# A streaming-encoder block on one Trainium2 core: where the moving operands begin in SBUF

## The chip, the core and the metric

One core of a Trainium2 chip runs the whole block as one program. The engines are TensorE (PE, with its weight loads listed as PEld), VectorE (DVE), ScalarE (ACT), GpSimd (POOL) and SyncE (SP), which issues most transfers. Each has its own queue of instructions, and they meet at semaphores. The metric is the device time of one execution in microseconds.

## The reference, cut to what matters

One layer on x of 512 tokens by 1024 features, all in float32:

```python
x = x + 0.5 * swiglu(rms_norm(x, ffn1_norm), w1, w3, w2)          # D_FF = 2816
h = rms_norm(x, mix_norm);  p = h @ w_in                           # 5288 columns
y_a = rwkv7_mixer(token_shift(p_rwkv), ...) @ rwkv_proj            # 8 heads x 64, delta rule
y_b = fox_mixer(p_fox, ...) @ fox_proj                             # 8 heads x 64, forgetting attention
x = x + (sigmoid(g_a) * y_a + sigmoid(g_b) * y_b) @ w_out
x = x + 0.5 * swiglu(rms_norm(x, ffn2_norm), v1, v3, v2)
out = rms_norm(x, final_norm)
# swiglu(h, w1, w3, w2) = (silu(h @ w1) * (h @ w3)) @ w2
```

## The kernel before, in words

Activations lie transposed: a tile holds 128 features by 512 tokens, so one product has a weight tile of 128 x 128 as the stationary operand and 512 columns of activations as the moving one. To keep float32 accuracy, every weight and every activation is split in two float32r parts, hi and lo, and `mm3` (L124 to L127) makes three products of each pair: weight hi with activation hi (L125), weight hi with activation lo (L126), weight lo with activation hi (L127).

Weights come through a ring of buffers: `raw` (three, filled by SP's queue, 512 KB at a time), `whi` (two, made by ACT, L117) and `wlo` (two, made by DVE, L118). These buffers and the normed activations `xh`, `xl` begin at byte 288 modulo 512 in each partition. One weight buffer holds eight tiles of 512 bytes per partition, so that every 128-column tile in it begins at 288 modulo 512 too.

The stages, by the names of the PSUM tiles that the products write:

- FFN 1 (`ffn`): `pa` and `pb` are h @ w1 and h @ w3 for each of 22 blocks of features, with `xh`/`xl` moving. DVE and ACT make silu(a) * b and split it into `hh` and `hl`. Then `pd`, the second product with w2: per output block m, 22 weight tiles with `hh`/`hl` moving, 66 products.
- The mixer: `pl` are the low-rank codes (72 and 96 weight columns instead of 128), `pk` the RWKV columns, `pgt` the gates, `pv` the values (here the weights move), `pq` the attention's q and k. The delta rule runs in chunks of 32 tokens as small fp32 products (`gp`, `xps`, `ups`, `sps`, `yps`) between the larger ones. Attention uses `lp`. LayerNorm over heads uses `yc` and `pg`.
- `ppj` (function `proj`): first the attention's output `yh`/`yl` by fox_proj, then the RWKV output `ya` by rwkv_proj, 96 products each. DVE gates the results, in the slots `G` and `ga`, with gate values that POOL's queue brings back from DRAM (`gsave`, L910 and L918). `pw` is the merged result `mh`/`ml` by w_out, 192 products; its sum goes to the reloaded residual `xS`.
- FFN 2 as FFN 1; its last output block is worked in two halves of 256 tokens with the weight buffers `ownh`/`ownl`, so that the final norm of one half runs beside the other (`ot`, `os`).

Buffers are laid out by pools, one behind the other in each partition: the constants `cp` first, then `xp` (activations), `wp` (weights), `tp` (temporaries), and behind these either `hp` (`hh`, `hl`) or the mixer's `rp` and `sp`. Pools opened with `side="right"` (`vtp`, `t2`) grow down from the other end. The order of the work is set by the tile framework's scheduler from the program text.

Where the operands begin, modulo 512, in the program before:

| buffers | used in | begin at |
|---|---|---|
| `whi`, `wlo`, `own`, `xh`, `xl` | weights everywhere; moving in `pa`, `pb`, `pk`, `pgt`, `pq`, `pl` | 288 |
| `hh`, `hl` | moving in `pd` | 416 |
| `yh`, `yl` | moving in the first `ppj` | 480 |
| `ya` | moving in the second `ppj` | 320 |
| `mh`, `ml` | moving in `pw` | 320 |
| `qa`, `kb`, `klc`, `vt`, `tr`, `pts` | attention | 480 (every second head's slice of `vt`: 224) |
| `la`, from which the first `qb` is made | attention, beside `klc` | 64 |
| `G`, `BK`, `RD`, `Tall`, `V4` (and the slots `ga`) | the recurrence, gates | 320 (every second chunk of `G` and `BK`: 64) |

Of the kernel before, what the change touches and what calls it, by code (L numbers as in the profile page):

```python
# [9 lines left out]
F32 = mybir.dt.float32  # L10
# [8 lines left out]
P = 128  # L19
T = 512  # L20
# [5 lines left out]
NP = DA // P  # L26
C = 32
NC = T // C
NB = T // P
# [6 lines left out]
PAR_W0, PAR_A0, PAR_KK, PAR_KA, PAR_RK, PAR_LG, PAR_LB = 38, 42, 46, 50, 54, 58, 62  # L36
PAR_Q, PAR_K, PAR_F = 66, 67, 68
PAR_N = 69

COL_W = 3 * DA  # L40
COL_G = COL_W + 64
# [9 lines left out]
def kernel(  # L51
# [7 lines left out]
    dve, act, pool, pe = nc.vector, nc.scalar, nc.gpsimd, nc.tensor  # L59

    cp = ctx.enter_context(tc.tile_pool(name="cp", bufs=1))
    xp = ctx.enter_context(tc.tile_pool(name="xp", bufs=1))
    wp = ctx.enter_context(tc.tile_pool(name="wp", bufs=2))
    tp = ctx.enter_context(tc.tile_pool(name="tp", bufs=4))
# [5 lines left out]
    def bank(name, pool_=None):  # L70
        pool_ = pool_ or pm
        return pool_.tile([P, T], F32, tag="b", name=name)

    def tmp(name, shape=(P, T), dt=F32, tag="t", **kw):
        return tp.tile(list(shape), dt, tag=tag, name=name, **kw)
# [3 lines left out]
    make_identity(nc, ident)  # L79
    identb = cp.tile([P, P], BF16, name="identb")  # L80
    dve.tensor_copy(identb[:], ident[:])
    ones = cp.tile([P, P], F32, name="ones")
    dve.memset(ones[:], 1.0)
    onesr = cp.tile([P, P], F32R, name="onesr")
    dve.tensor_copy(onesr[:], ones[:])
    bones = tmp("bones", (P, P))
    dve.memset(bones[:], 0.0)
    dve.memset(bones[0:64, 0:64], 1.0)
# [115 lines left out]

    par = cp.tile([P, PAR_N], F32, name="par")

# [5 lines left out]
    nc.scalar.dma_start(g1[:], ffn1_norm[0].rearrange("(a b) -> a b", b=P))  # L212
    warm = bank("warm", pf)
    for _ in range(8):
        pe.matmul(warm[:, 0:P], ones[:], ones[:], start=True, stop=True)
    gtp = bank("gtp", pr)
    pe.transpose(gtp[:, 0:8], g1[:], ident[0:8, 0:8])
    dve.tensor_copy(par[:, 0:8], gtp[:, 0:8])
# [28 lines left out]
    tc.keep_in_program_order(pin)  # L247
    rows = rtp.tile([PAR_N, P], F32, name="rows")
    loraw = rtp.tile([P, DA], F32, name="loraw")
# [45 lines left out]
    def place_params():  # L295
        ptp = bank("ptp")
        pe.transpose(ptp[:, 0:PAR_N], rows[:], ident[0:PAR_N, 0:PAR_N])
        dve.tensor_copy(par[:, 8:PAR_N], ptp[:, 8:PAR_N])
        dve.tensor_scalar(par[:, PAR_Q:PAR_Q + 1], par[:, PAR_Q:PAR_Q + 1], 0.125, None, op0=ALU.mult)
# [79 lines left out]
    with ExitStack() as mx:  # L379
        rp = mx.enter_context(tc.tile_pool(name="rp", bufs=1))  # L380
# [13 lines left out]

        nka = rp.tile([P, NP], F32, name="nka")
        dve.tensor_scalar(nka[:], par[:, PAR_KA:PAR_KA + NP], -1.0, None, op0=ALU.mult)
        tiny = rp.tile([P, 2], F32, name="tiny")
        dve.memset(tiny[:, 0:1], 1e-24)
        dve.memset(tiny[:, 1:2], -1e-24)
        omu = rp.tile([P, PAR_W0 - PAR_MU], F32, name="omu")  # L400
        dve.tensor_scalar(omu[:], par[:, PAR_MU:PAR_W0], -1.0, 1.0, op0=ALU.mult, op1=ALU.add)

        def shifted(o, src, rows, mu):
            act.activation(o[0:rows, :], src[0:rows, :], AF.Copy, scale=omu[0:rows, mu - PAR_MU:mu - PAR_MU + 1])
            dve.scalar_tensor_tensor(o[0:rows, 1:T], src[0:rows, 0:T - 1], pc(mu)[0:rows, :], o[0:rows, 1:T],
                                     op0=ALU.mult, op1=ALU.add)
# [47 lines left out]
        xctx.close()  # L454
        fctx = ExitStack()
        vtp = fctx.enter_context(tc.tile_pool(name="vtp", bufs=1, side="right"))
        pctx = ExitStack()
        t2 = pctx.enter_context(tc.tile_pool(name="t2", bufs=1, side="right"))
        cmask = t2.tile([P, T], F32, name="cmask")
        pool.memset(cmask[:], 1.0)  # L460
        pool.memset(cmask[:].rearrange("p (c t) -> p c t", t=C)[:, :, 0:1], 0.0)

        PC = rp.tile([P, NP, NC], F32, name="PC")
        Ld = dp.tile([P, C, C], F32, name="Ld")
        Td = dp.tile([P, C, C], F32, name="Td")
        V4 = rp.tile([P, NP, T], F32, name="V4", tag="V4")
# [37 lines left out]
        def step(p):  # L504
# [21 lines left out]
            with tc.issue_after(logs.ins):  # L526
                act.activation(Pi[:], cz[:], AF.Exp, scale=DEC)
                act.activation(Pp[:, :, 1:C + 1], ch(cz), AF.Exp, scale=-DEC)
            pool.tensor_copy(PC[:, p, :], Pp[:, :, C])
            dve.tensor_tensor(BK[:, :, 1, :], ch(k), ch(Pi), op=ALU.mult)  # L530
# [87 lines left out]
        for i in range(2):  # L618
            for q in range(2):
                o = i * 64 + q * C  # L620
# [6 lines left out]
        def half(q):  # L627
            return slice(q * 64, (q + 1) * 64)
# [49 lines left out]
        vt = []  # L678
# [6 lines left out]
                    mm3(vps[b][:], mix.hi[kk][:, bs], mix.lo[kk][:, bs], wh[:, k, :], wl[:, k, :],  # L685
                        kk == 0, kk == KD - 1)
        for b in range(NB):
            o = vtp.tile([P, T], F32, name=f"vt{b}", tag=f"vt{b}")
            act.activation(o[:], vps[b][:], AF.Copy, scale=rc[:, b:b + 1])
            vt.append(o)  # L690
        plain_gate(NP)
# [10 lines left out]
        for q in range(2):  # L702
            pool.memset(Rs[0][half(q), :, q, :], 0.0)
            for i in range(4):
                o = (1 - q) * 64
# [21 lines left out]
        for c in range(NC):  # L727
# [3 lines left out]
            for p, q in heads():  # L731
                o = (p // 2) * 64 + q * C
# [12 lines left out]
            if c + 1 < NC:  # L745
# [3 lines left out]
                for q in range(2):  # L749
                    decay = dve.tensor_tensor(Rn[half(q), :, q, :], sps[half(q)],  # L750
                                      PC[half(q), :, c:c + 1].broadcast_to([64, NP, 64]), op=ALU.mult)
            holes += [hx, hx, hu, hu, hs, hs]
# [21 lines left out]
        for q in range(2):  # L774
            o = (1 - q) * 64
            pool.memset(f32(klc[q][:]), 0.0)
            dve.tensor_copy(klc[q][o:o + 8, :], fz[FR, :])
        for q in range(2):
            o = (1 - q) * 64
# [8 lines left out]
        for p in range(NP):  # L788
            qp, kp = qks[p]
            qa = [t2.tile([P, T], F32R, tag=f"qa{q}", name=f"qa{q}") for q in range(2)]  # L790
            kb = [t2.tile([P, T], F32R, tag=f"kb{q}", name=f"kb{q}") for q in range(2)]


            for q in range(2):
                h_, g_ = half(q), half(1 - q)
                h = 2 * p + q
                act.copy(qa[q][h_, :], qp[h_, :])
                dve.tensor_tensor(qa[q][g_, :], qp[h_, :], f32(qa[q][h_, :]), op=ALU.subtract)
                dve.tensor_copy(kb[q][h_, :], kp[h_, :])
                dve.tensor_copy(kb[q][g_, :], kp[h_, :])  # L800
                dve.tensor_tensor(klc[q][h_, :], kp[h_, :], f32(kb[q][h_, :]), op=ALU.subtract)
                act.copy(qb[q][h_, :], qp[h_, :])
                dve.tensor_copy(qb[q][g_, :], sel[g_, h:h + 1].broadcast_to([64, T]))
            mx_ = [tp.tile([P, 2 * NB], F32, tag=f"mx{q}", name=f"mx{q}", bufs=2) for q in range(2)]
            for i, bl in enumerate(((0, 1), (2,), (3,))):
                at = {b: sum(c + 1 for c in bl[:j]) * P for j, b in enumerate(bl)}
                w = sum(b + 1 for b in bl) * P
                lps, trs = [], []
                for q in range(2):
                    lp = pf.tile([P, T], F32, tag="b", name="lp")  # L810
                    lps.append(lp)
                    for b in bl:
                        n, bs = (b + 1) * P, slice(b * P, (b + 1) * P)
                        l = lp[:, at[b]:at[b] + n]
                        pe.matmul(l, qa[q][:, bs], kb[q][:, 0:n], start=True, stop=False)
                        pe.matmul(l, qb[q][:, bs], klc[q][:, 0:n], start=False, stop=False)
                        pe.matmul(l[:, b * P:n], identb[:], dmask[:], start=False, stop=True)
                for q in range(2):
                    pt, mx = pts[:, q], mx_[q]
                    for b in bl:  # L820
                        n, mb = (b + 1) * P, mx[:, b:b + 1]
                        l = lps[q][:, at[b]:at[b] + n]
                        dve.tensor_reduce(mb, l, axis=AX.X, op=ALU.max, negate=True)
                        act.activation(pt[:, at[b]:at[b] + n], l, AF.Exp, bias=mb, accum_out=mx[:, NB + b:NB + b + 1])
                    sb_ = mx[:, NB + bl[0]:NB + bl[-1] + 1]
                    dve.reciprocal(sb_, sb_)
                    for b in bl:
                        v = pt[:, at[b]:at[b] + (b + 1) * P]
                        dve.tensor_scalar(v, v, mx[:, NB + b:NB + b + 1], None, op0=ALU.mult)
                for q in range(2):  # L830
                    tpp = lps[q]
                    for k in range(w // P):
                        pe.transpose(tpp[:, k * P:(k + 1) * P], pts[:, q, k * P:(k + 1) * P], ident[:])
                    tr = t2.tile([P, T], F32, tag="tr", name="tr", bufs=2)
                    act.copy(tr[:, 0:w], tpp[:, 0:w])
                    trs.append(tr)

                av = lps[1]
                for j, b in enumerate(bl):
                    for k in range(b + 1):  # L840
                        o = at[b] + k * P
                        for q in range(2):
                            h = 2 * p + q
                            pe.matmul(av[half(q), j * P:(j + 1) * P], vt[k][:, h * 64:(h + 1) * 64],
                                      trs[q][:, o:o + P], start=k == 0, stop=k == b)
                dve.tensor_copy(qp[:, bl[0] * P:(bl[-1] + 1) * P], av[:, 0:len(bl) * P])
                if p == 0 and i < 2:
                    load_qk(i + 2, holes)
                    norm_qk(i + 2)
                elif 3 * p + i < 3 * NP - 1:  # L850
                    early(3 * p - 2 + i)
            yb.append(qp)
# [50 lines left out]
        for p in range(NP):  # L903
            o = vtp.tile([P, T], F32R, name=f"yh{p}", tag=f"vt{p}")
# [119 lines left out]
```

## Time and profile before

| | |
|---|---|
| median of three timed runs | 1213.7 us |
| lowest and highest of them | 1209.55 and 1213.95 us |
| span of the profiled execution, first to last instruction | 1210.2 us |
| mean granted TensorE clock in it | 0.992 |
| TensorE busy | 1184.5 us, 98% |
| DVE, ACT, POOL busy | 665.2, 458.1, 100.5 us |
| moved by DMA | 122.54 MB, 101 GB/s in the mean |

The page and the views give times from the start of the span; for the profiled execution there is no other time than this span. "Busy" of TensorE is the union of its products: a product of 512 columns stands with some 390 ns from its start to its modelled end, while the next one starts some 230 ns after it. The time that a stream of products costs is therefore read from start to start. The granted clock stands as a share of full speed.

### The profile page before, as it was taken

The page shows a single profiled execution, that of the slowest core. Times are in us where ns is not written, and L with a number is a line of the kernel's source. Part 1 is how long each engine was busy: PE and PEld are TensorE (multiplying, and loading weights), DVE is VectorE, ACT ScalarE, POOL GpSimd, SP SyncE. Part 2 cuts the span into 40 slices and gives each one's busy share as a digit, 9 for nine tenths or more (in the row PEclk, how much of TensorE's full clock was granted, in tenths as well). Part 3 has the DMA queues.
Part 4 walks back from the last instruction along what each step waited for, and adds up shares of the span by engine and source line. Part 5 has one row for each costly group of instructions (what it writes and reads, how often), then busy time and mean ns, then how long its engine had stood idle before and what let it go on. Part 6 is the DMA issues. An engine that isn't in the chain of part 4 may idle for free.

```text
span 1210.2 us, 15874 instructions
## 1 busy us (share of the span) xinstructions
PE 1184.5 (98%) x6334; PEld 955.1 (79%) x6334; DVE 665.2 (55%) x993; ACT 458.1 (38%) x739; POOL 100.5 (8%) x144
## 2 busy tenths in 40 slices
PE   8999999999999999999999999999999999999997
PEld 6788888888887788887667777678888888888887
DVE  7454555443443688776766666865554445443232
ACT  5222222222222854445867655523322222222221
POOL 4100000001111111321000011111000000000110
PEclk9999999999999999999999999999999999999999
DMA  6233233333334234345113235532333333323331
GB/s 186 73 95 105 87 105 88 104 95 108 107 111 106 76 104 124 109 135 131 36 36 102 63 97 163 178 106 87 103 102 92 100 104 88 104 80 96 96 96 70
DMA packets 208152, 122.54 MB, mean 101 GB/s; under 512 B 9902, under 2 KB 200430, under 8 KB 208078
## 3 DMA queue, kind: packets, MB, share of 16 engines
q1 hardware_dynamic: 202078, 108.67, 31.1%
q0 software_dynamic: 3760, 12.06, 3.2%
q8 instruction: 50, 0.82, 0.3%
q10 hardware_dynamic: 2240, 0.79, 0.3%
q14 instruction: 24, 0.20, 0.1%
HBM read 110.82 MB, written 10.68 MB: 100 GB/s over the span
## 4 chain that ended last, share of the span: by engine, by line
PE 93%; DVE 3%; ACT 1%; issue 0%; DMA 0%; DVEq 0%; POOL 0%; POOLq 0%
PE pd L127 7%; PE pd L125 7%; PE pd L126 7%; PE pa L125 7%; PE pa L126 7%; PE pa L127 6%; PE pb L127 6%; PE pb L126 6%; PE pb L125 6%; PE pgt L125 3%; PE pgt L127 2%; PE pgt L126 2%; PE pk L125 2%; PE pk L127 2%; PE pk L126 2%; PE pw L127 1%
## 5 line engine op out<-in xcount | busy, mean ns | idle before, releaser
L117 ACT CAST whi<-raw 128x1024 fp32r<-128x1024 f32 (+3 forms) x199 | 198.2, 998 | 631.2 <-PE pa L126 180.7
L118 DVE TENSOR_TENSOR wlo<-raw,whi 128x1024 fp32r<-128x1024 f32 (+2 forms) x198 | 229.5, 1159 | 142.3 <-ACT whi L117 142.2
L125 PE MATMUL pa<-xh,whi 128*128 128x512 f32 x344 | 134.7, 392 | 2.6 <-DVE fa L326 2.6
L127 PE MATMUL pb<-xh,wlo 128*128 128x512 f32 x344 | 134.5, 391 | 0.9 <-DVE wlo L118 0.9
L126 PE MATMUL pa<-xl,whi 128*128 128x512 f32 x344 | 134.6, 391 | 0.0
L125 PE MATMUL pb<-xh,whi 128*128 128x512 f32 x344 | 134.5, 391 | 0.0
L126 PE MATMUL pb<-xl,whi 128*128 128x512 f32 x344 | 134.5, 391 | 0.0
L127 PE MATMUL pa<-xh,wlo 128*128 128x512 f32 x344 | 134.4, 391 | 0.0
L127 PE MATMUL pd<-hh,wlo 128*128 128x512 f32 x330 | 130.8, 396 | 0.0
L125 PE MATMUL pd<-hh,whi 128*128 128x512 f32 x330 | 130.3, 395 | 0.0
L126 PE MATMUL pd<-hl,whi 128*128 128x512 f32 x330 | 130.3, 395 | 0.0
L330 DVE TENSOR_TENSOR fb<-pb,rstd 128x512 f32<-128x512 f32 x43 | 29.7, 691 | 137.5 <-PE pb L127 137.5
L125 PEld LDWEIGHTS pa<-xh,whi 128*128 128x128 f32 x344 | 64.9, 189 | 16.7 <-DVE fa L326 3.1
L127 PEld LDWEIGHTS pb<-xh,wlo 128*128 128x128 f32 x344 | 65.0, 189 | 14.8 <-DVE wlo L118 1.3
L127 PEld LDWEIGHTS pa<-xh,wlo 128*128 128x128 f32 x344 | 65.0, 189 | 13.6
L126 PEld LDWEIGHTS pa<-xl,whi 128*128 128x128 f32 x344 | 65.0, 189 | 13.5
L126 PEld LDWEIGHTS pb<-xl,whi 128*128 128x128 f32 x344 | 65.0, 189 | 13.5
L125 PEld LDWEIGHTS pb<-xh,whi 128*128 128x128 f32 x344 | 64.9, 189 | 13.5
L126 PEld LDWEIGHTS pd<-hl,whi 128*128 128x128 f32 x330 | 62.0, 188 | 14.9
L125 PEld LDWEIGHTS pd<-hh,whi 128*128 128x128 f32 x330 | 62.0, 188 | 14.6
L127 PEld LDWEIGHTS pd<-hh,wlo 128*128 128x128 f32 x330 | 62.0, 188 | 14.6
L326 DVE TENSOR_TENSOR fa<-pa,rstd 128x512 f32<-128x512 f32 x43 | 29.7, 692 | 73.6 <-PE pa L127 73.6
(395 smaller groups left out, 1968.0 us busy)
## 6 DMA issues: line engine op xcount, KB each, us to landing
raw<-in_ffn_w_dram SPq DMA_DIRECT2D x118, 512.0 KB
raw<-in_w_in_dram SPq DMA_DIRECT2D x40, 512.0 KB
raw<-in_ffn_w_dram SPq DMA_DIRECT2D x15, 384.0 KB
raw<-in_w_out_dram SPq DMA_DIRECT2D x8, 512.0 KB
gsave<-gs SPq DMA_DIRECT2D x9, 256.0 KB
xin<-in_x_dram SPq DMA_DIRECT2D x4, 512.0 KB
xsave<-xT POOLq DMA_DIRECT2D x8, 256.0 KB, 2.3
G<-gsave POOLq DMA_DIRECT2D x8, 256.0 KB, 3.8
```

The source lines that it names most:

```text
L117: act.copy(hi[:], raw[:])
L118: (eng or dve).tensor_tensor(lo[:], raw[:], hi[:].bitcast(F32), op=ALU.subtract)
L125: pe.matmul(ps, whi, xhi, start=first, stop=False)
L126: pe.matmul(ps, whi, xlo, start=False, stop=False)
L127: return pe.matmul(ps, wlo, xhi, start=False, stop=last)
L326: dve.tensor_tensor(a[:], pa[:], nrm.rstd[:], op=ALU.mult)
L330: dve.tensor_tensor(b[:], pb[:], nrm.rstd[:], op=ALU.mult)
```

## The change

The arithmetic and its operands stay the same; what changes is where buffers begin.

- The constant matrix `ones` (512 bytes per partition) is no longer kept: it is a temporary for the first products and for making `onesr`, the float32r copy. Later uses of `ones` read `onesr`, whose values are the same 1.0.
- `mx0` and `mx1`, two buffers each, grow from 32 to 128 bytes (`PAD` = 32 elements). With the 512 bytes that fell out, everything behind them begins 128 bytes lower: `hh`/`hl` go from 416 to 288.
- In the mixer's pool `tiny` grows to 128 bytes and `PC` (256 bytes) is placed before `la` and not behind it. `V4`, `G`, `BK`, `RD`, `Tall`, and so `ya`, `mh` and `ml`, go from 320 to 288; `la` from 64 to 288.
- On the right side, the four `vt` tiles are named when their pool opens, and a pad of 192 bytes, `vtpad`, follows. The attention's tiles and `yh`/`yl` go from 480 to 288; the temporaries of the RWKV steps (`khi`, `klo`, `u`) from 416 to 224.

`whi`, `wlo`, `xh` and `xl` stay at 288, and the matrices `ident`, `bonesr` and `center` stay where they were modulo 512. On each engine the instructions, their order and their waits are those of before.

```diff
+PAD = 32
...
-    ones = cp.tile([P, P], F32, name="ones")
-    dve.memset(ones[:], 1.0)
+    ones_ = tmp("ones", (P, P))
+    dve.memset(ones_[:], 1.0)
     onesr = cp.tile([P, P], F32R, name="onesr")
-    dve.tensor_copy(onesr[:], ones[:])
+    dve.tensor_copy(onesr[:], ones_[:])
+    ones = onesr[:].bitcast(F32)
...
-        pe.matmul(warm[:, 0:P], ones[:], ones[:], start=True, stop=True)
+        pe.matmul(warm[:, 0:P], ones_[:], ones_[:], start=True, stop=True)
...
-        tiny = rp.tile([P, 2], F32, name="tiny")
+        tiny = rp.tile([P, PAD], F32, name="tiny")
...
+        PC = rp.tile([P, NP, NC], F32, name="PC")
...
+        vts = [vtp.tile([P, T], F32, name=f"vt{b}", tag=f"vt{b}") for b in range(NB)]
+        vtp.tile([P, 48], F32, name="vtpad", tag="vtpad")
...
-        PC = rp.tile([P, NP, NC], F32, name="PC")
...
-            o = vtp.tile([P, T], F32, name=f"vt{b}", tag=f"vt{b}")
+            o = vts[b]
...
-            mx_ = [tp.tile([P, 2 * NB], F32, tag=f"mx{q}", name=f"mx{q}", bufs=2) for q in range(2)]
+            mx_ = [tp.tile([P, PAD], F32, tag=f"mx{q}", name=f"mx{q}", bufs=2) for q in range(2)]
```

## The prediction

> **What bounds the kernel now.** I read the page's first part first, then its chain that ended last, then the groups of instructions. The page says:
>
> ```profile
> span 1210.2 us, 15874 instructions
> PE 1184.5 (98%) x6334; PEld 955.1 (79%) x6334; DVE 665.2 (55%) x993; ACT 458.1 (38%) x739; POOL 100.5 (8%) x144
> ...
> PE 93%; DVE 3%; ACT 1%; issue 0%; DMA 0%; DVEq 0%; POOL 0%; POOLq 0%
> ```
>
> TensorE is busy 98% of the span and carries 93% of the chain, so the span is close to a sum over its products. What a product costs there is not its "mean ns": products are pipelined, and the next starts while the last still runs. The groups of whole 512-column products show two kinds all the same:
>
> ```profile
> L126 PE MATMUL pa<-xl,whi 128*128 128x512 f32 x344 | 134.6, 391 | 0.0
> ...
> L126 PE MATMUL pd<-hl,whi 128*128 128x512 f32 x330 | 130.3, 395 | 0.0
> ```
>
> Same shape and type, neither ever idle, yet 4 ns apart. `pa` and `pb` are the first FFN products (moving `xh`, `xl`, which begin at byte 288 modulo 512, as the weights do), `pd` the second (moving `hh`, `hl`, at 416). The cost that counts is the time from start to start. I take it from the view by windows for TensorE alone, where the bracket behind the busy time is its count; two windows that begin together cancel the products cut at an edge:
>
> ```profile
> core 0: us, PE busy (x), PEclk, DMA share, GB/s
> 140.00:180.00 40.00, 40.00 (x178) 1.00 0.33 96
> 140.00:260.00 120.00, 120.00 (x531) 1.00 0.33 96
> 265.00:305.00 40.00, 40.00 (x173) 1.00 0.36 109
> 265.00:385.00 120.00, 120.00 (x516) 1.00 0.37 108
> ```
>
> `pa`/`pb`: 80 us hold 531 - 178 = 353 products, **226.6 ns** each. `pd`: 80 us hold 516 - 173 = 343, **233.2 ns** each. TensorE is busy all the time in both and the clock is granted in full, so the 6.6 ns are neither a wait nor a throttle.
>
> Is it the starting byte, or the stage? The other stages with matching and with unlike starts tell, by the first and last row of a stretch of the timeline and the count of the window:
>
> ```profile
> 540.00:559.00 19.00, 19.00 (x86) 1.00 0.45 127
> 740.20:745.50 5.30, 5.30 (x24) 1.00 1.04 319
> 807.00:815.00 8.00, 8.00 (x36) 1.00 0.41 119
> 539.71 0.39 PE L125 MATMUL pq<-xh,whi 128*128 128x512 f32 x1
> ...
> 558.98 0.39 PE L126 MATMUL pq<-xl,whi 128*128 128x512 f32 x1
> 739.97 0.39 PE L886 MATMUL yc<-yklc,center 128*128 128x512 f32 x1
> ...
> 745.33 0.40 PE L126 MATMUL ppj<-yl,whi 128*128 128x512 f32 x1
> 806.77 0.39 PE L126 MATMUL pw<-ml,whi 128*128 128x512 f32 x1
> ...
> 814.93 0.40 PE L127 MATMUL pw<-mh,wlo 128*128 128x512 f32 x1
> ```
>
> `pq`, with `xh`/`xl` in the middle of the mixer (288 against 288): 19.27 us / 85 = 226.7 ns. The projection `ppj` (480 against 288): 5.36 / 23 = 233.0 ns. `pw`, the product with w_out (320 against 288): 8.16 / 35 = 233.1 ns. So three kinds of unlike start (128, 192 and 32 bytes apart) give 233, and like starts give 226.6, in stages whose DMA share runs from 0.33 to 1.04; DMA and the other engines' load do not sort them. The nearest to a test within one set of moving buffers is `pl`, whose moving operands are `xh`/`xl` too, but whose weight tiles are 72 or 96 columns wide and so begin at ten different multiples of 32:
>
> ```profile
> 394.64 0.40 PE L127 MATMUL pl<-xh,wlo 128*96 128x512 f32 x1
> ...
> 396.48 0.40 PE L126 MATMUL pl<-xl,whi 128*96 128x512 f32 x1
> ```
>
> Nine rows, 8 intervals in 1.84 us: 230 ns with the buffers that run at 226.7 against whole weight tiles. It points the same way, less cleanly, since the tiles are also narrower.
>
> By a rule of the Trainium skill the starting byte should not matter at all: "SBUF — State Buffer", section "Who interferes with whom", gives TensorE two independent read ports, one for the moving operand and one for the weight load, and says that it never waits on anyone. By that rule the time would stay as it is, which is the first rival below; the 233.2 against 226.6 ns of equal, never idle products disagree with it.
>
> **The change part by part.** On every engine the instructions and their waits stand in the same order before and after; only addresses differ. So nothing is queued differently, and the sum is products times nanoseconds saved.
>
> 1. `pd` with 512 columns: 3 x 330 = 990 products (the page's rows), 416 to 288. Saved 990 x (233.2 - 226.6) = **6.5 us**. That the other engines keep up is shown by `pa`/`pb`: they need the same weight bytes per product and more passes of DVE, and hold 226.6 ns from 140 to 260 us.
> 2. `pd` with 256 columns, the last output tile, 3 x 44 = 132 products:
>
> ```profile
> 1189.00:1193.00 4.00, 4.00 (x36) 1.00 0.00 0
> 1188.75 0.36 PE L125 MATMUL pd<-hh,ownh 128*128 128x256 f32 x1
> 1188.95 0.28 PE L126 MATMUL pd<-hl,ownh 128*128 128x256 f32 x1
> ...
> 1192.97 0.28 PE L127 MATMUL pd<-hh,ownl 128*128 128x256 f32 x1
> ```
>
> 36 rows, the first of them the one after the transposes: 4.02 us / 34 = 118.2 ns. No 256-column product with like starts is to be read cleanly in this trace. Bounds: nothing gained (the loss is per weight load, and cannot shrink at half the width), or half of 6.6 ns twice over, 6.6 ns each, 0.9 us. I take 118.2 - 226.6/2 = 4.9 ns, estimated from the two rows, so **0.65 us**.
> 3. `ppj`, two projections of 96 products (480 and 320 to 288), and `pw`, 192 (320 to 288). At 6.4 ns: 192 x 6.4 = 1.2 us each. `pw` is paced by TensorE (busy 8.00 of 8 us above), so I keep **1.2 us**. For `ppj` part of it falls into waits (the last row is of all engines: TensorE's products, its weight loads, DVE, ACT, POOL):
>
> ```profile
> PE ppj L125 <- ACT whi L117: 1.6, 1, 1.6
> PE ppj L125 <- ACT ya L143: 0.7, 1, 0.7
> 763.00:788.00 25.00, 22.78 (x95) 17.13 (x94) 19.80 (x31) 15.52 (x25) 3.47 (x7) 1.00 0.67 208
> ```
>
> The chain of LayerNorm and split that makes `ya` runs on ACT and DVE beside the first 96; if it is what ends last there, their 0.6 us turn into a longer wait for `ya`. In the second 96 DVE is at 19.80 of 25 us, near its own bound but not on it. Bounds 0 and 1.2; I take the half, **0.6 us**.
> 4. Attention's small products, `pn`, `pz`, the transposes and the fp32 products of the recurrence: their two operands move by the same number of bytes, or stay unlike, but for half of the `klc` products, 16 of them. At 6.6 ns that is 0.1 us at most: **0**. The time of the recurrence is waits and latency, which addresses leave alone.
> 5. DVE, ACT and DMA on moved buffers. DVE's rows of one form are equal whether the buffer begins at 288 (`fb`) or at 320 (`ga`), 691 against 685 ns:
>
> ```profile
> L330 DVE TENSOR_TENSOR fb<-pb,rstd 128x512 f32<-128x512 f32 x43 | 29.7, 691 | 137.5 <-PE pb L127 137.5
> L941 DVE TENSOR_TENSOR ga<-ga,G 128x512 f32<-128x512 f32 x7 | 4.8, 685 | 0.0
> ```
>
> **0**, with 6 ns over some 40 such passes (0.2 us, under TensorE's cover) as the far bound. The dropped constant costs a copy nowhere: `onesr` was made before, and `ones` now reads it.
>
> Sum: 6.5 + 0.65 + 1.2 + 0.6 = **9.0 us**, 0.74% of the profiled 1210.2 us, which gives 1201.2 us for an execution like it. The three timed runs have a median of 1213.7 us (1209.55 to 1213.95), 3.5 us over the profiled span, which lies near the lowest. From the median: 1213.7 - 9.0 = **1204.7 us**. By the bounds of 2, 3 and 4 the saving lies between 7.7 and 10.0.
>
> One thing moves this without any cause in the edit. The granted clock falls to half for short spells:
>
> ```profile
> 27.00:31.00 4.00, 3.51 (x9) 0.60 0.81 237
> 37.00:41.00 4.00, 3.75 (x10) 0.63 0.45 131
> 412.00:416.00 4.00, 3.48 (x10) 0.69 0.50 131
> 627.00:631.00 4.00, 3.23 (x19) 0.70 0.00 0
> 850.00:1070.00 220.00, 220.00 (x972) 1.00 0.33 97
> ```
>
> In each of four spells 0.30 to 0.40 of 4 us is lost, 1.2 to 1.6 us, and all lie beside starts and waits, none in the 220 us of the densest stream (972 products). A tighter stream therefore should not bring more, but everything after the first `pd` stage now comes 3.4 us earlier, so a spell may come or go: 1.6 us either way, and about two of them are the spread of the runs.
>
> **The rivals.**
> - *The starting byte is not the cause* (what `pd`, `ppj` and `pw` share would then be something else, such as freshly made operands that are read after long use of the others). For it: the change shifts nothing else, and every slow stage but `pl` has moving buffers other than `xh`/`xl`. Against it: `pl` at 230 ns with `xh`/`xl`. Then nothing is saved: 1213.7 us.
> - *The stream closes up only part of the way*, to the 230 ns of `pl`, where 3 of the 16 weight tiles begin at 288 too: (233.2 - 230) x (990 + 192 + 96) = 4.1 us, 1209.6 us. For it: `pl` itself. Against: whole streams of like starts hold 226.6 over 353 products.
> - *Slower: transfers to the moved slots.* `gsave` comes back to `G` and `ga` on POOL's queue; these slots go from a multiple of 64 bytes (320) to an odd multiple of 32 (288), as `xS` (480) already has:
>
> ```profile
> G<-gsave POOLq DMA_DIRECT2D x8, 256.0 KB, 3.8
> ga<-gsave POOLq DMA_DIRECT2D x8, 256.0 KB, 4.1
> xS<-xsave POOLq DMA_DIRECT2D x8, 256.0 KB, 6.2
> 744.03 0.55 POOL L910 DMA_DIRECT2D G<-gsave  x1 [1.77 <-DVE G L912]
> 751.77 0.40 PE L125 MATMUL ppj<-yh,whi 128*128 128x512 f32 x1
> ```
>
> If that is why `xS` takes 6.2 us, 16 transfers gain 2.1 to 2.4 us each: 16 x 2.4 = 38 us if none were covered, 1243 us. But the last `G` is issued at 744.03 and needed when its `ppj` is done, about 752: landing after 3.8 it has some 4 us to spare, so it decides only from about 4 us more per transfer. And `xS` is issued eight at once, so each waits for those ahead.
>
> **How the numbers follow.** Forecast 0.78; no effect 0.12; part of the way 0.07; slower 0.03. The likeliest gives 1204.7 us; its own range is 1213.7 less 7.7 to 10.0, widened by 3 us for the clock spells and the spread of runs: 1200.5 to 1209. For 8 in 10 with room for the partial case and a median among the lower runs: 1198 to 1211. What a measurement can tell from no change is about 0.5%, 6 us, so faster means under 1207.6. The forecast lies 3 us within that, so 0.05 of its 0.78 falls to "same", and the partial case goes there almost whole: faster 0.75, same 0.22, slower 0.03.
>
> **What would show it.** By windows of 80 us inside the two `pd` stages: 353 products where there were 343 (right), 343 (first rival), about 348 (second). The mean of `pd<-hl,whi` falls from 395 to 391 ns, those of `pw` and `ppj` likewise, and `pa`, `pb`, `pq` stay. The first `pd` stage, from 262 to 385 us, shortens and the mixer starts 3.4 us earlier, with its own length unchanged. Step 3 is wrong if the waits for `ya` do not grow and the whole 1.2 us appears; step 5 if DVE's 685 ns or the landing of `G` and `ga` move. The prediction fails as a whole if `pd` reads 226.6 and the span does not shrink by at least 7 us: then a wait elsewhere took the gain.

## The result, and the profile after the change

The changed kernel takes **1202.6 us** (median; 1200.3 to 1205.1) against 1212.2 us (1209.6 to 1214.0) for the kernel before, timed in turn on the same chip: a ratio of **0.992**, 95% interval 0.990 to 0.994. It is faster by some 9.6 us; the forecast was 1204.7 us, by a saving of 9.0 us.

The page of the changed kernel still shows a kernel that is one long stream of products. Its profiled execution took 1205.1 us in all, 1.8 us more than its span, and was the longest of its four. By the same difference the profiled execution of the kernel before, with a span of 1210.2 us, would have taken about 1212.0 us, near its median (an estimate from these two figures).

```profile
span 1203.3 us, 15874 instructions
PE 1176.3 (98%) x6334; PEld 955.7 (79%) x6334; DVE 664.9 (55%) x993; ACT 458.2 (38%) x739; POOL 100.5 (8%) x144
L128 PE MATMUL pa<-xl,whi 128*128 128x512 f32 x344 | 134.6, 391 | 0.0
L128 PE MATMUL pd<-hl,whi 128*128 128x512 f32 x330 | 128.5, 389 | 0.0
```

The counts are those of before: 6334 products, 330 of the second FFN kind. TensorE is busy 8.2 us less (1184.5 before), and the other engines within 0.4 us of what they were. `pd<-hl,whi` fell from a mean of 395 to 389 ns; `pa<-xl,whi` stayed at 391.

The view by windows for TensorE alone (start and end, length, busy time with its count, granted clock, DMA share, GB/s) counts products in the same two stretches as before:

```profile
140.00:180.00 40.00, 40.00 (x178) 1.00 0.32 93
140.00:260.00 120.00, 120.00 (x531) 1.00 0.33 96
265.00:305.00 40.00, 40.00 (x178) 1.00 0.36 109
265.00:385.00 120.00, 120.00 (x531) 1.00 0.38 110
```

The first FFN products (`pa`, `pb`) keep their 353 products in 80 us. The second FFN products (`pd`) now have 531 - 178 = 353 as well, where there were 343: 226.6 ns from start to start instead of 233.2.

**Where the 8 us went.** The timeline gives the start of the first product of each stage. Before:

```profile
8.37 1.07 PE L231 MATMUL xtp<-ident,xin 128*128 128x128 f32 x8 [1.35 <-DMA xin<-in_x_dram]
...
262.17 0.40 PE L125 MATMUL pd<-hh,whi 128*128 128x512 f32 x1
...
385.37 0.39 PE L125 MATMUL pl<-xh,whi 128*72 128x512 f32 x1
...
733.11 0.50 PE L125 MATMUL ppj<-yh,whi 128*128 128x512 f32 x1 [0.19 <-DVE gs L633]
...
788.34 0.39 PE L125 MATMUL pw<-mh,whi 128*128 128x512 f32 x1
...
834.77 0.39 PE L125 MATMUL pa<-xh,whi 128*128 128x512 f32 x1
...
1074.65 0.40 PE L125 MATMUL pd<-hh,whi 128*128 128x512 f32 x1
...
1181.10 0.28 PE L125 MATMUL pd<-hh,ownh 128*128 128x256 f32 x1
...
1203.64 0.36 PE L986 MATMUL os<-ones,sq 128*128 128x1 f32 x2
```

After:

```profile
9.18 1.94 PE L233 MATMUL xtp<-ident,xin 128*128 128x128 f32 x8 [2.99 <-DMA xin<-in_x_dram]
...
263.35 0.39 PE L127 MATMUL pd<-hh,whi 128*128 128x512 f32 x1
...
383.03 0.40 PE L127 MATMUL pl<-xh,whi 128*72 128x512 f32 x1
...
730.57 0.50 PE L127 MATMUL ppj<-yh,whi 128*128 128x512 f32 x1 [0.20 <-DVE gs L638]
...
785.05 0.39 PE L127 MATMUL pw<-mh,whi 128*128 128x512 f32 x1
...
830.27 0.39 PE L127 MATMUL pa<-xh,whi 128*128 128x512 f32 x1
...
1070.13 0.39 PE L127 MATMUL pd<-hh,whi 128*128 128x512 f32 x1
...
1174.10 0.28 PE L127 MATMUL pd<-hh,ownh 128*128 128x256 f32 x1
...
1196.68 0.36 PE L991 MATMUL os<-onesr,sq 128*128 128x1 f32 x2
```

Taking each stage as the time from its first row to the next row:

| stage | before, us | after, us | saved | forecast |
|---|---|---|---|---|
| up to the first `pd` | 262.17 | 263.35 | -1.18 | 0 |
| `pd`, first FFN | 123.20 | 119.68 | 3.52 | 528 x 6.6 ns = 3.5 |
| mixer, `pl` to the first `ppj` | 347.74 | 347.54 | 0.20 | 0 |
| projections `ppj` | 55.23 | 54.48 | 0.75 | 0.6 |
| `pw` and what follows it | 46.43 | 45.22 | 1.21 | 1.2 |
| first products of the second FFN | 239.88 | 239.86 | 0.02 | 0 |
| `pd`, second FFN, 512 columns | 106.45 | 103.97 | 2.48 | 446 x 6.6 ns = 2.9 |
| `pd` with 256 columns, and the last 16 with 512 | 22.54 | 22.58 | -0.04 | 0.65 + 0.11 |
| sum | 1203.64 | 1196.68 | 6.96 | 9.0 |

The stages that the change touches give back 8.1 us; the first row takes 1.2 away again. That row is no part of the change: its first wait, for the input `xin`, is 1.35 us in one execution and 2.99 in the other. In the profiled executions of the experiments below the same wait lies between 1.4 and 2.9 us, whatever was edited. The two spans differ by 6.9 us and the medians by 9.6, mostly since the execution profiled after the change lies 2.4 us above its median.

### The profile page after: what moved, and what is told of

It is laid out like the page before. It is cut to its first block, busy times and chain, and to the rows that moved or that the text cites. A ratio compares the mean times of both kernels' runs of the same rounds, so it can differ in the third digit from the quotient of the medians.

```text
span 1203.3 us, 15874 instructions
## 1 busy us (share of the span) xinstructions
PE 1176.3 (98%) x6334; PEld 955.7 (79%) x6334; DVE 664.9 (55%) x993; ACT 458.2 (38%) x739; POOL 100.5 (8%) x144
## 4 chain that ended last, share of the span: by engine, by line
PE 93%; DVE 3%; ACT 1%; issue 0%; DVEq 0%
PE pd L128 7%; PE pd L129 7%; PE pd L127 7%; PE pa L127 7%; PE pa L128 7%; PE pb L128 7%; PE pa L129 7%; PE pb L129 7%; PE pb L127 7%; PE pgt L127 3%; PE pgt L128 2%; PE pgt L129 2%; PE pk L129 2%; PE pk L127 2%; PE pk L128 2%; PE pw L129 1%
```

## The experiments

All edits are against the changed kernel, in which weights (`raw`, `whi`, `wlo`) and moving operands begin at byte 288 modulo 512. They move buffers and leave the order of the instructions on every engine as it is. "Triple" is the three products of `mm3`: hi weights with the hi operand, hi weights with the lo operand, lo weights with the hi operand; "alike" and "unlike" say whether the moving operand begins at the weights' byte.

### 1. Move the weights away, and 2. move everything together

The weights alone go to 160, so that every weight product has unlike operands, those of the first FFN products and of the mixer too:

```
     def load_raw(aps, kt, n):
     ...
+    wp.tile([P, 96], F32, tag="wpad", name="wpad", bufs=1)
...
-            mx_ = [tp.tile([P, PAD], F32, ...
+            mx_ = [tp.tile([P, 2 * NB], F32, ...
```

> Only the weight buffers move: a pad of 384 bytes ahead of the ring puts raw, whi and wlo at 160 modulo 512; mx0 and mx1 go back to 32 bytes, so that everything behind the ring, hh, ya, mh included, stays at 288, as xh and xl do. All 4446 products of 512 columns with a streamed weight tile are then unlike by 128 bytes; only the 132 of 256 columns (own buffers, 288) stay alike. Theory (the difference between the two starts counts): pa, pb, pd, pq all at about 233 ns, 80 us of them hold 343 products instead of 353; 4446 x 6.6 = 29 us more, of which some 3 vanish in waits of the mixer: 1202.6 + 26 = 1229 us, ratio to the kernel before 1.014. Rival (the place or the making of hh, ya, mh was the cause, not the difference): all spacings stay at 226.6, 1203 us.

And everything together to 416, so that all stay alike at another byte:

```
     sel = cp.tile([P, 8], F32, name="sel")
+    cp.tile([P, 32], F32, name="cpad")
...
-        vtp.tile([P, 48], F32, name="vtpad", tag="vtpad")
+        vtp.tile([P, 16], F32, name="vtpad", tag="vtpad")
```

> A pad of 128 bytes behind the constants moves weights and moving operands together: whi, wlo, xh, hh, ya, mh, yh all begin at 416 modulo 512 instead of 288, and the right side follows. Theory (only the difference counts): pa, pb and pd stay at 226.6 ns, 1202.6 us within the spread of the runs (1200 to 1205). Rival (a place modulo 512 is good in itself, 288, and 416 is bad): all streams at 233, about 1229 us.

With the weights at 160 the kernel takes **1226.7 us** (1225.3 to 1228.7), 1.013 of the kernel before (1.011 to 1.015) and 24.0 us more than the changed one (23.4 more than the kernel with all at 416, timed in the same turn). With all at 416 it takes **1203.3 us**, 0.993 (0.992 to 0.995), as the changed kernel does. The windows of the kernel with its weights at 160:

```profile
140.00:180.00 40.00, 40.00 (x174) 1.00 0.33 96
140.00:260.00 120.00, 120.00 (x518) 1.00 0.32 94
265.00:305.00 40.00, 40.00 (x173) 1.00 0.38 112
265.00:385.00 120.00, 120.00 (x518) 1.00 0.37 107
```

344 products in 80 us in the first FFN stage, which the change never touched and which held 353: 232.6 ns against 226.6. The second stretch holds 345, 231.9 ns. The groups of the changed kernel have 1482 triples of this shape; 4446 products by some 5.7 ns, the mean of the two stretches, are 25 us, and 24.0 are measured. With all at 416 both stretches hold 353. So neither the byte itself nor the buffer or the stage decides, but whether both operands of a product begin alike. The first rival (the starting byte is not the cause) is out.

### 3. Undo the FFN part alone

```
             (in the second FFN products, ahead of hh and hl)
+            hp.tile([P, 32], F32, name="hpad")
```

> The changed kernel with the FFN part alone undone: a pad of 128 bytes ahead of hh and hl in both FFNs puts them back to 416; the mixer and the projections keep the change. Theory: pd back at 233.2 ns, 990 x 6.6 = 6.5 us more, 1209 us; the last output block of 256-column products unchanged at 120 ns; pw and ppj stay at 226.6. Rival (the gain came from elsewhere, or is only partly that of pd): less than 3 us more, 1205 us or under.

**1209.7 us** (1207.6 to 1211.7), 0.998 of the kernel before (0.997 to 0.999): what is left without the FFN part is 0.17%, 2.1 us (0.7 to 3.4). The timeline had 0.20 + 0.75 + 1.21 = 2.2 us for mixer, `ppj` and `pw`. The FFN part, 1209.7 - 1202.6, is 7.1 us; the timeline had 3.52 + 2.48 = 6.0, and in the trace of this run the two `pd` rows are 6.1 us longer than in the changed kernel. The difference of 1 us is within what the runs scatter.

### 4. Only the lo weights unlike

What does an unlike weight tile slow down, the product that uses it or the one that runs while it is loaded? With `wlo` alone at 160, one product in three has an unlike weight tile.

```
 (in split_w)
             hi = wp.tile([P, kt, n], F32R, tag="whi", name="whi", bufs=2)
+            if not wpad:
+                wpad.append(wp.tile([P, 96], F32, tag="wpad", name="wpad", bufs=1))
             lo = wp.tile([P, kt, n], F32R, tag="wlo", name="wlo", bufs=2)
...
-            mx_ = [tp.tile([P, PAD], F32, ...
+            mx_ = [tp.tile([P, 2 * NB], F32, ...
```

> Only wlo moves, to 160 modulo 512; whi and all moving operands stay at 288. In each triple (whi with xh, whi with xl, wlo with xh) one weight tile of three is unlike. Theory A (the moving stream collides with the load of the NEXT weight tile, which runs beside it): the product before the unlike load, L-line of whi with the lo activations, takes some 233 ns to the next start, the other two 226.6. Theory B (a product collides with its own weight tile): the wlo product itself takes 233, the others 226.6. For either 1482 x 6.6 = 9.8 us more, 1212 us. Theory C (one unlike tile breaks the whole stream up, as pl in the trace before suggests): all three at 230 to 233, 1217 to 1231 us.

**1219.6 us** (1218.6 to 1221.4), 1.006 (1.005 to 1.008): slower than the kernel before, and far from the 1212 of one slow product in a triple. The groups of the first FFN stage, from 140 to 260 us, show which (L131 is the first product of the triple, L133 the one with `wlo`):

```profile
L133 PE MATMUL pa<-xh,wlo 128*128 128x512 f32 x86 | 34.1, 397 | 0.0
L132 PE MATMUL pa<-xl,whi 128*128 128x512 f32 x86 | 34.1, 396 | 0.0
L131 PE MATMUL pa<-xh,whi 128*128 128x512 f32 x86 | 33.5, 389 | 0.0
```

The first product keeps 389 ns; the second, alike in itself, and the third are slow. By the mean from start to start the three are 226.7, 232.5 and 234.1 ns, 13.4 ns more per triple than three times 226.67. 1482 triples by 13.4 ns are 19.9 us; 17.0 are measured, and that the stages with waits take up the rest is argued, not measured. The timeline of all engines shows when the unlike tile is loaded (PEld):

```profile
199.95 0.40 PE L132 MATMUL pb<-xl,whi 128*128 128x512 f32 x1
199.95 0.19 PEld L133 LDWEIGHTS pb<-xh,wlo 128*128 128x128 f32 x1
```

The load starts with the second product and takes 0.19 us of the 0.23 until the next start. So both are slow: the product during which the unlike tile is loaded, and the one that uses it.

### 5, 6. How far is unlike? 32, 64, 256 and 384 bytes

The pad ahead of `hh` and `hl` gets another size, one for the first FFN and one for the second:

```
+            hp.tile([P, 16 if final is not None else 8], F32, name="hpad")     (5: 32 bytes, then 64)
+            hp.tile([P, 96 if final is not None else 64], F32, name="hpad")    (6: 256 bytes, then 384)
```

> As the experiment that undoes hh, but hh and hl begin 32 bytes past the weights (320) in the first FFN and 64 bytes past (352) in the second. Theory (any unlike multiple of 32 modulo 512 is slow): pd at 231 to 234 ns in both FFNs, 6.5 us more than the changed kernel, 1209 us. Rival (the distance counts, or the modulus is smaller than 512): one of the two stays at 226.6, and 3 us are missing.

> The same with 256 bytes past the weights (hh at 32) in the first FFN and 384 (160) in the second. Theory: pd at 231 to 234 ns in both, 1209 us. Rival (a modulus of 256 or 128): the first FFN at 226.6 (and the second, for 128), 1206 or 1203 us.

Read by the stage, not by the sum (1209.2 and 1204.2 us, a single run each). The windows of the first FFN's `pd`, 32 bytes apart:

```profile
265.00:305.00 40.00, 40.00 (x173) 1.00 0.37 109
265.00:385.00 120.00, 120.00 (x516) 1.00 0.37 106
```

and 256 bytes apart:

```profile
265.00:305.00 40.00, 40.00 (x178) 1.00 0.37 109
265.00:385.00 120.00, 120.00 (x531) 1.00 0.39 113
```

32 bytes cost as much as 128 (343 products, 233.2 ns); 256 bytes cost nothing (353, 226.6 ns). In the second FFN 384 bytes, which is 128 beyond 256, gave 233 ns, and 64 bytes about 229. So the effect repeats after 256 bytes, at the two distances tried, and not only after the 512 that the change was made by.

### 7. Only the lo operand unlike

The mirror of the fourth: all `hh` at 288, all `hl` at 416.

```
+            his = [hp.tile([P, T], F32R, name=f"hh{j}") for j in range(KF)]
+            hp.tile([P, 32], F32, name="hpad")
+            los = [hp.tile([P, T], F32R, name=f"hl{j}") for j in range(KF)]
...
-                hi = hp.tile([P, T], F32R, name=f"hh{j}")
-                lo = hp.tile([P, T], F32R, name=f"hl{j}")
+                hi, lo = his[j], los[j]
```

> Only hl moves, to 416; hh and both weight rings stay at 288. One product of three in pd (weight hi with hl) has an unlike moving operand. Theory AB, from the run with wlo moved (a product is slow where its moving operand is unlike its own tile, or unlike the tile that is loaded meanwhile): only that product slow, 234 ns, the two others 226.7, 687 ns for three, 330 x 7.3 = 2.4 us more, 1205 us. Rival (each unlike operand within a triple costs it 13.4 ns, as wlo did: 693.4 against 680): two of the three slow, 693 ns for three, 4.4 us more, 1207 us.

1206.4 us (a single run), between the two. The groups of the first FFN's `pd`, 265 to 380 us; then two groups of the second FFN's `pd`, first from 1071 to 1089 us and then from 1092 to 1105 us:

```profile
L128 PE MATMUL pd<-hl,whi 128*128 128x512 f32 x168 | 66.4, 395 | 0.0
L127 PE MATMUL pd<-hh,whi 128*128 128x512 f32 x168 | 65.4, 389 | 0.0
L129 PE MATMUL pd<-hh,wlo 128*128 128x512 f32 x168 | 65.2, 388 | 0.0
...
L129 PE MATMUL pd<-hh,wlo 128*128 128x512 f32 x27 | 10.5, 388 | 0.0
L127 PE MATMUL pd<-hh,whi 128*128 128x512 f32 x26 | 10.1, 389 | 0.0
...
L127 PE MATMUL pd<-hh,whi 128*128 128x512 f32 x19 | 7.5, 397 | 0.0
L129 PE MATMUL pd<-hh,wlo 128*128 128x512 f32 x19 | 7.5, 392 | 0.0
```

In the first FFN only the product that moves `hl` is slow: 226.7, 234.2 and 225.8 ns from start to start. That fits the fourth: the tile loaded while `hl` moves is slow for that same product, and its neighbours have `hh`. In the second FFN, taken whole, all three are slow, 231 to 232 ns each, though the bytes modulo 512 are the same. But it begins as the first does. Its `pd` stream is interrupted six times by four transposes (`ot`), at 1090.21 us for the first time. Until then the three take 227, 234 and 226 ns; behind that interruption they take 236, 234 and 230, and behind later ones between 227 and 235, with the pattern changing at the transposes. The same kernel was run once more (the eleventh run) to see whether the difference of the FFNs was chance:

> The run with hl alone moved, repeated, since its two FFNs differed (686.7 ns for three products in the first, some 694 in the second). If the two patterns belong to the stages: 687 and 694 again. If a stream settles by chance in one of two patterns: any other pairing.

1206.9 us, with the same values in both FFNs, and in the second the same pace behind each interruption, to 0.1 ns in the mean. So it is not chance, and it does not belong to the stage as a whole: what the second FFN has and the first has not is the interruptions. With unlike starts the stream can settle at another pace behind each of them; with like starts (the changed kernel) it comes back to 226.7 ns behind all six. Why an interruption sets the pace stays open.

### 8. Bring the rest alike

Is there more to be had? The constants that are multiplied by (`ident`, `onesr`, `center`, `bonesr`) are put at 288, and the narrow weight tiles of `pl` are padded so that all of them begin there:

```
-            hi = wp.tile([P, kt, n], F32R, tag="whi", name="whi", bufs=2)
-            lo = wp.tile([P, kt, n], F32R, tag="wlo", name="wlo", bufs=2)
+            hi = wp.tile([P, kt, max(n, P)], F32R, tag="whi", name="whi", bufs=2)[:, :, 0:n]
+            lo = wp.tile([P, kt, max(n, P)], F32R, tag="wlo", name="wlo", bufs=2)[:, :, 0:n]
     (and the small constants allocated ahead of ident)
```

> The changed kernel with the rest made alike: the small constants stand first, so that ident, onesr, center and bonesr begin at 288 too, and weight tiles of 72 and 96 columns are stored 128 columns apart, so that pl's tiles all begin at 288. Theory: pl falls from 231 to 227 ns (48 products, 0.2 us), ssum, pq's sums, pg and yc likewise (38 products, 0.2 us), transposes by 0 to 3 ns each (208 of them, 0 to 0.6 us): 0.4 to 1 us less than the changed kernel, 1202 us, ratio to the kernel before 0.991 to 0.993, not to be told apart from the change by its time alone. Rival (pl is slow for its narrow tiles and not for their starts): pl stays at 230 to 232.

1203.6 us (1202.9 to 1204.9), 0.993 (0.992 to 0.995): no further gain. And `pl` stays near where it was; the timeline, nine rows, of which the first and the last:

```profile
390.86 0.39 PE L128 MATMUL pl<-xh,whi 128*96 128x512 f32 x1
...
392.70 0.39 PE L130 MATMUL pl<-xh,wlo 128*96 128x512 f32 x1
```

8 intervals in 1.84 us, 230 ns, with every operand alike. Over all 48 products of `pl` the mean is 230.4 ns, against 232.2 in the changed kernel and 231.4 in the kernel before. So at most some 2 ns hang on its starts, and it does not come near 226.6. That the narrow tiles are the reason is what is left over; no run tests it.

### 9, 10. 64 and 192 bytes, 16 and 224 bytes

```
+            hp.tile([P, 48 if final is not None else 16], F32, name="hpad")    (9: 64 bytes, then 192)
...
+            hall = hp.tile([P, 2 * KF * T + 64], F32R, name="hall")            (10: 16 bytes, then 224)
+            off = 4 if final is None else 56
...
-                hi = hp.tile([P, T], F32R, name=f"hh{j}")
-                lo = hp.tile([P, T], F32R, name=f"hl{j}")
+                hi, lo = [hall[:, off + (2 * j + i) * T:off + (2 * j + i + 1) * T] for i in range(2)]
```

> hh and hl 64 bytes past the weights (352) in the first FFN and 192 past (480) in the second. Theory now (period of 256 bytes, from 226.6 ns at 256 and 233 at 384): slow at both, 233 at 192, and at 64 either 233 or the 229 that the second FFN showed at this distance. In the first FFN 80 us of pd hold 343 products (233) or 349 (229). Rival (64 bytes slow only beside the transposes of the second FFN, like otherwise): 353 products, 226.6.

> All of hh and hl lie in one buffer, so that they can begin 16 bytes past the weights (304) in the first FFN, and 224 past (0) in the second. Theory (any difference modulo 256 is slow): 233 in both, 343 products in 80 us of the first FFN. Rival (steps of 32 bytes are what is told apart): 226.6 and 353 products at 16, 233 at 224. A third outcome, under 226 ns, would mean that equal starts are not the best ones.

1205.4 and 1209.8 us, a single run each. The windows of the first FFN's `pd`, 64 bytes apart:

```profile
265.00:305.00 40.00, 40.00 (x176) 1.00 0.37 109
265.00:385.00 120.00, 120.00 (x526) 1.00 0.38 110
```

and 16 bytes apart:

```profile
265.00:305.00 40.00, 40.00 (x174) 1.00 0.36 109
265.00:385.00 120.00, 120.00 (x520) 1.00 0.38 109
```

350 products at 64 bytes, 228.6 ns; 346 at 16 bytes, 231.2 ns. A count in 80 us is good to one product, 0.7 ns; the mean from start to start in the timeline is 228.9 and 231.7 ns. So even 16 bytes cost some three quarters of the whole, 64 bytes only a third, in the first FFN as in the second (experiment 5, 229.1). 192 and 224 bytes in the second FFN cost the whole, 233 ns, by the mean from start to start without the intervals at the transposes. No distance came below 226.6 ns. Together, modulo 256 (the last two by the mean, the others by counts):

| distance, bytes | 0 (and 256) | 16 | 32 | 64 | 128 (and 384) | 192 | 224 |
|---|---|---|---|---|---|---|---|
| ns per 512-column product | 226.6 | 231.2 | 233.2 | 228.6 | 233.2 | 233.3 | 233.2 |

The 256-column products at the end of the second FFN tell another story. Their rows, first and last of 35, with `hh` and `hl` alike (the changed kernel):

```profile
1181.90 0.28 PE L128 MATMUL pd<-hl,ownh 128*128 128x256 f32 x1
...
1185.96 0.28 PE L129 MATMUL pd<-hh,ownl 128*128 128x256 f32 x1
```

and 192 bytes on (experiment 9):

```profile
1182.91 0.28 PE L128 MATMUL pd<-hl,ownh 128*128 128x256 f32 x1
...
1186.77 0.28 PE L129 MATMUL pd<-hh,ownl 128*128 128x256 f32 x1
```

4.06 us / 34 = 119.4 ns for the operands that begin alike, 3.86 / 34 = 113.5 ns with the moving ones 192 bytes on, and 118.2 at 128 bytes (the kernel before). For them "alike" is no advantage at all.

## Why the prediction was right, point by point

**What bounds the kernel** held: the span is close to a sum over products, and the time from start to start, read by counting in windows, was the quantity that moved. Nothing behind TensorE took the gain: where the stream tightened, DVE, ACT and the DMA queues kept up.

**Step 1**, `pd` with 512 columns, was 6.5 us and measured 6.0. The first FFN gave 3.52 of 3.5 us. The second gave 2.48 of 2.9: 2.48 us over the 446 products of that row are 5.6 ns each and not 6.6. The 6.6 had been read in the first FFN alone and carried over to the second, whose stream is interrupted six times by the transposes. In the changed kernel the five to nine products behind each interruption take mostly 228 to 236 ns before the pace of 226.7 returns; without the intervals at the interruptions the mean of the row is 227.1 ns. In the kernel before it is 232.8 and not 233.2. These 0.4 + 0.4 ns of 432 products, and the 12 intervals at the interruptions, which did not shorten, make up the missing 0.4 us.

**Step 2**, 256 columns, 0.65 us, failed. It carried a rate per column over to another shape, by a guess between two rows; the measured saving of that row is -0.04 us, at the lower bound of 0. Like starts did not help these products: they took 119.4 ns instead of 118.2, and ran fastest when 192 bytes apart. The step said that the trace had no such product with like starts to read; the bound of 0 was the better value.

**Step 3**: `pw` gave 1.21 of 1.2 us. `ppj` gave 0.75 where 0.6 was taken from bounds of 0 and 1.2. The reason for the half was that the missing part would turn into a longer wait for `ya`. The waits of the changed kernel's `ppj` (total, count, longest, in us):

```profile
PE ppj L127 <- ACT whi L119: 1.6, 1, 1.6
PE ppj L127 <- ACT ya L145: 0.7, 1, 0.7
```

At this resolution they are what they were, 1.6 and 0.7. The timeline has the wait for `ya` at 0.66 us before and 0.75 after, and one interval between two products near 777 us is 0.08 us longer, without a wait that the profile names. So the mechanism given for the half is there, with some 0.15 of the missing 0.45 us. The rest is a thing that the step did not have: `yc`, `pg` and the waits interrupt this stream too, and in the products just behind an interruption the changed kernel is no faster than the one before. That the half came out near was in good part luck.

**Steps 4 and 5** held. The mixer gained 0.20 us where at most 0.1 was allowed for its products, within what two executions differ by. DVE's passes and the transfers to the moved slots did not change (the group of DVE, and a row of the DMA issues whose last column is the us to landing):

```profile
L946 DVE TENSOR_TENSOR ga<-ga,G 128x512 f32<-128x512 f32 x8 | 5.5, 685 | 0.0
...
G<-gsave POOLq DMA_DIRECT2D x8, 256.0 KB, 3.7
```

685 ns as before, and 3.7 us against 3.8, with the slot now at an odd multiple of 32. `ga` lands after 4.2 us (4.1 before) and `xS` after 6.2 as it did, so the start of the slot was not why `xS` takes longer: the third rival is out.

**The evidence from `pl` was misread.** The prediction took its 230 ns as a sign for the starting bytes, "less cleanly". Experiment 8 put all its starts alike and it stayed at 230 ns, so that row said next to nothing on the question, and the size of the second rival, read from it, had no ground. What carried the case was the other comparison, `pq` against `ppj` and `pw`, and experiments 1 and 2 bear it out.

**The rule of the Trainium skill** cited in the prediction ("SBUF — State Buffer", section "Who interferes with whom": two independent read ports on TensorE, which never waits on anyone) would have left the time as it was, as the prediction applied it; that the starting byte does not matter was the prediction's inference. For the time of these products the measurement differs: 226.6 ns with like starts, 232.6 with the weights moved by 128 bytes, and 24 us on the kernel. Whether it is the two reads that wait for each other was not shown.

**The total** came out nearer than its parts: 9.0 was forecast, the touched stages gave 8.1 in the profiled executions, and the medians differ by 9.6, which the interval of the ratio puts between 6.9 and 12.0 us. So the mechanism was right, and that 9.0 lies so close to 9.6 is partly luck. One reading in it was wrong: it compared run times with a span and took the profiled execution before to lie near the lowest. A run's time is some 1.8 us longer than its span (1205.1 against 1203.3), which puts that execution near the median. The forecast, taken from the median of the runs, did not depend on it.

## What to carry to other kernels

When a kernel is one dense stream of products, count the starts in equal windows of stages that should be equal; a difference of 3% there was worth more here (some 8 us in the touched stages) than any single wait that is left (the longest is 3.0 us, for `xin`). For float32r products of 512 columns let moving buffers and weight buffers begin alike modulo 256 bytes, and check a suspected layout effect by moving the buffers that the edit did not touch: moving only the weights cost 24 us, moving everything together nothing, and these two runs settled the cause. Compare a like shape only: `pl`, with its narrow tiles, and the 256-column products did not follow the rule of the 512-column ones.

## What the runs showed of the hardware that was not expected

- The effect repeats after 256 bytes: 226.6 ns at 256 apart, 233 at 128 and at 384.
- It is finer than 32 bytes: 16 bytes apart cost some 5 ns of the 6.6. And it does not grow evenly: 64 bytes apart cost some 2.
- One unlike weight tile slows two products, the one during which it is loaded and the one that uses it, 13.4 ns per triple; one unlike moving operand slowed only its own product (7.6 ns) as long as the stream ran without interruption, and all three behind the first interruption.
- An interruption by a few transposes leaves its mark on a dense stream: with like starts some five to nine products take mostly 228 to 236 ns before the pace of 226.7 returns, with unlike ones the stream can settle at another pace (experiment 7: 228.9 ns in the mean of the triple, then 233.3 or 231.1).
- Products of 256 columns do not gain from like starts: 119.4 ns alike, 118.2 at 128 bytes apart, 113.5 at 192.
- Why two reads that begin alike should go faster together was not shown; that the reads of a moving operand and of the weights loaded beside it meet somewhere is argued from experiment 4, where the load runs beside the product that it slows, and not measured. Distances under 16 bytes and the weights of the 256-column products moved alone were not tried.
